# Transposing attention queries and keys before their split into two parts

## The chip, the cores and the metric

The kernel runs on one core of a Trainium2 chip. The metric is the device time of one execution in microseconds; the median of the runs shown for the kernel before is 2201.02 us.

## The reference

One trunk layer of a streaming encoder, in float32, for 2048 prompt frames and 64 frames of a running stream (2112 tokens, width 1024):

```python
a = _rmsnorm(hp, norm1)
z = a @ w_in                                   # 1024 x 2816: q, k, v of attention; q, k, v, gate of retention
qa, ka = rotate(8 heads x 64), rotate(2 kv heads x 64)
attn_o = softmax(qa ka^T / 8, with a sink per head) va    # a frame reads chunks c-2, c-1, c of 64 frames
ret_o  = chunkwise retention (4 heads x 128, decay per head)
hp = hp + concat(attn_o, rmsnorm(ret_o) * silu(gate)) @ w_out
hp = hp + relu(rmsnorm(hp) @ w_up) ** 2 @ w_down
y  = _rmsnorm(hp, norm_f)
```

It also returns the newest keys and values and the retention state of both streams. The decode stream's keys are a cache of 128 frames followed by its own 64.

## The kernel before, in words

Matrix products run on TensorE (PE) in the fast format `float32r`. To keep the precision of float32, an operand is split into a high part (a copy into float32r, on ACT) and a low part (the value less its high part, on DVE), and a product is three matmuls: high by high, high by low, low by high.

The kernel has two stretches. The first, some 730 us, does projection, attention and retention; the second the output projection and the MLP. The change is in the first. It runs over two groups `ph` of attention and retention heads (4 query heads, 1 key head and 2 retention heads each), and in each over 17 tiles of tokens: 16 of 128 and the 64 of the decode stream; 34 tiles in all. For each tile there are three projections: `z0` (384 columns: values 64, queries 256, keys 64), `z1` (512: queries and keys of the retention) and `z2` (512: its values and gates). Each is eight steps `k` of three matmuls (L584, L585, L587).

Behind each projection a first stage takes the result out of PSUM. For attention that is `att_a`: DVE and POOL rotate queries and keys into the tile `zr` [tokens, 6 blocks of 64: value, 4 queries, key] (L249), and then the whole of `zr` is split into `hl` (L254 to L256), where the high and the low part of each block stand beside each other. `vd` (L260, L261) holds copies of the split values for the scores' overlapping part.

The other stages of a tile run on PE in between the projection steps of later ones:

- `att_b` transposes `hl`: four transposes into the bank `pq` (one per query head; 128 columns are high and low part, so that the transposed head has the high part in 64 partitions and the low in the other 64), which ACT copies to `qT`; and two transposes into the bank `pk` in `keys` (high over low and low over high), which ACT copies to `kw`, the key window of this tile, and DVE to the first half of `kw_next`, that of the next tile. For the decode tile the cache's keys are split in `cache_prep` and transposed too.
- `att_c` multiplies `qT` by the two forms of `kw` (scores `s`), takes the maximum (DVE, `mx`, `ngm`) and the exponentials (ACT, L317; L321 is the sink's), and divides (DVE, L329).
- `att_d` transposes the probabilities, `idf` being the float32 identity, and splits them when it reads the banks `pt` and `pm`. `att_e` multiplies by the values, with high and low part of the values as the two halves of the stationary operand.
- `ret_b` transposes the rotated queries and keys of the retention (bank `ptr`, in float32), which DVE (`rqT`) and then ACT (`rkT`) read. `ret_c` multiplies them (`pss`). `ret_d` and `ret_e` follow.

The order of PE and of SP's queue is written out when the program is built: `run_ready` keeps a clock that counts the cost of projection steps (3 x columns x 0.4237 ns) and of stages (`COST`). A stage becomes due a time `LAT` after the stage that it needs, longer by a factor `slow` for some tiles at the ends, and is put in at the first projection step at which it is due. So `LAT` says how long ACT, DVE and POOL are trusted to take. The wait itself is done by semaphores: if they take longer, PE stands still. The order of ACT, DVE and POOL, each of which runs its instructions in a fixed order, is found by the scheduler of the framework when it builds. Two engines that read one PSUM bank do it one after the other.

Of the kernel before, what the change touches and what calls it, by code (L numbers as in the profile page):

```python
# [24 lines left out]
NT = SEQ // 128 + 1  # L25
# [14 lines left out]
def body(ctx, tc, xt, xd, xtok, w1, wout, wup, wdn, gains, sinks, ck, cv, sret, rot, rdec, qdec, dmask,  # L40
         yT, nkp, nvp, nrp, nks, nvs, nrs):
    nc = tc.nc
# [13 lines left out]
    idf = cp.tile([128, 128], F32, name="idf")  # L56
    make_identity(nc, idf)
    idr = cp.tile([128, 128], F32R, name="idr")
# [31 lines left out]
    wk = late.enter_context(tc.tile_pool(name="wk", bufs=1))  # L90
# [49 lines left out]
    def tok(t):  # L140
        return t * 128, (128 if t < NT - 1 else DEC)
# [33 lines left out]
    last_act, last_dve = [None], [None]  # L175
# [25 lines left out]
    def psum(name, dt=F32):  # L201
        return pp.tile([128, 512], dt, name=name, tag="w")
# [19 lines left out]
    def new_kw():  # L222
        return wk.tile([128, 2, 256], F32R, name="kw", bufs=2)

    def new_hl():
        return wk.tile([128, 832], F32R, name="hl", bufs=3)

    def keys(hl, T, outs):

        pk = psum("pk", F32R)  # L230
        nc.tensor.transpose(pk[:, 0:T], hl[:T, 640:768], idr[:T, :T])
        nc.tensor.transpose(pk[:, 128:128 + T], hl[:T, 704:832], idr[:T, :T])
        src = pk[:, 0:256].rearrange("p (a t) -> p a t", a=2)[:, :, :T].bitcast(F32)
        for i, o in enumerate(outs):
            if i == 0:
                nc.scalar.activation(o, src, AF.Copy)
            else:
                nc.vector.tensor_copy(o, src)

    class Att:  # L240
        pass
# [1 line left out]
    def att_a(c, ph, t, z0, rt, kw, kw_next, hl_prev):  # L243
        t0, T = tok(t)
        c.ph, c.t, c.t0, c.T, c.kw, c.kw_next, c.hl_prev, c.nch = ph, t, t0, T, kw, kw_next, hl_prev, T // 64
        zr = wk.tile([128, 6, 64], F32, name="zr")
        cs = rt[:T, 0:128].rearrange("p (a d) -> p a d", a=2)
        nc.scalar.activation(zr[:T, 0], z0[:T, 0:64], AF.Copy, scale=rs[:T, t:t + 1])
        rotate(zr[:T, 1:6], z0[:T, 64:384].rearrange("p (b d) -> p b d", d=64), T, t, 5, 64, cs)  # L249
        hl = c.hl = new_hl()  # L250
        c.vd_prev = att[ph, t - 1].vd if 0 < t < NT - 1 else None
        vd = c.vd = wk.tile([128, 2, 128], F32R, name="vd", bufs=3)
        hv = hl[:T, :768].rearrange("p (b a d) -> p b a d", a=2, d=64)
        nc.scalar.activation(hv[:, :, 0], zr[:T], AF.Copy)  # L254
        last_act[0] = nc.scalar.activation(hl[:T, 768:832], zr[:T, 5], AF.Copy)
        last_dve[0] = nc.vector.tensor_sub(hv[:, :, 1], zr[:T], hv[:, :, 0].bitcast(F32))  # L256

        for a in range(c.nch):
            v = hl[64 * a:64 * a + 64, 0:128].bitcast(F32)
            nc.scalar.activation(vd[64 * (1 - a):128 - 64 * a, a], v, AF.Copy)  # L260
            nc.vector.tensor_copy(vd[64 * a:64 * a + 64, a], v)  # L261
        with tc.issue_after(last_pool[0].ins):
            if t == NT - 2:
                nc.gpsimd.dma_start(nkp[:, ph], zr[:, 5])
                nc.gpsimd.dma_start(nvp[:, ph], zr[:, 0])
            if t == NT - 1:
                nc.gpsimd.dma_start(nks[64:128, ph], zr[:T, 5])
                nc.gpsimd.dma_start(nvs[64:128, ph], zr[:T, 0])
            if ph == 0:
                token_rest(t)  # L270

    def att_b(c):
        T, nch, hl = c.T, c.nch, c.hl
        if c.t == NT - 1:
            keys(c.hl_prev, 128, [c.kw[:, :, 0:128]])
        pq = psum("pq", F32R)
        for j in range(4):
            nc.tensor.transpose(pq[:, j * 128:j * 128 + T], hl[:T, 128 + j * 128:256 + j * 128], idr[:T, :T])
        qT = c.qT = wk.tile([128, 2, 4, 64], F32R, name="qT")
        nc.scalar.activation(qT[:, :nch].rearrange("p c h q -> p h c q"),  # L280
                             pq.rearrange("p (h c q) -> p h c q", h=4, q=64)[:, :, :nch].bitcast(F32), AF.Copy)
        outs = [c.kw[:, :, 128:128 + T]]
        if c.kw_next is not None:
            outs.append(c.kw_next[:, :, 0:128])
        keys(hl, T, outs)

    def att_c(a):
        t, g, kw, qT, nch = a.t, a.ph, a.kw, a.qT, a.nch
# [42 lines left out]
    def att_d(a):  # L331


        a.parts = [[], []]
        n, t = a.nch, a.t
        full = [c for c in range(n) if c == 1 or t > 0]
        f0, f1 = full[0] * 256, full[-1] * 256 + 256
        K = 128 if n == 2 and t > 0 else 64
        pt, pm = psum("pt"), psum("pm")
        for c in full:  # L340
            for pr in range(2):
                v = 2 * c + pr
                nc.tensor.transpose(pt[:, v * 128:v * 128 + 128], a.p[:, pr, 256 * c:256 * c + 128], idf)
        for pr in range(2):
            nc.tensor.transpose(pm[:K, pr * 128:pr * 128 + 128], a.p[:, pr, 128:128 + K], idf)
        th = wk.tile([128, 512], F32R, name="ph")
        tl = wk.tile([128, 512], F32R, name="pl")
        tm = wk.tile([128, 2, 256], F32R, name="pm")
        nc.scalar.activation(th[:, f0:f1], pt[:, f0:f1], AF.Copy)
        nc.vector.tensor_sub(tl[:, f0:f1], pt[:, f0:f1], th[:, f0:f1].bitcast(F32))  # L350
        for c in full:
            vv = (a.hl if c else a.hl_prev)[:, 0:128]
            a.parts[c] += [(vv, x[:, 256 * c:256 * c + 256]) for x in (th, tl)]
        for c in range(K // 64):
            h, l = tm[64 * c:64 * c + 64, c], tm[64 * (1 - c):128 - 64 * c, c]
            x = pm[64 * c:64 * c + 64, 0:256]
            nc.scalar.activation(h, x, AF.Copy)
            nc.vector.tensor_sub(l, x, h.bitcast(F32))
            a.parts[c].append(((a.vd_prev if c else a.vd)[:, c], tm[:, c]))

    def att_e(a):
# [101 lines left out]
    def load_cache(ph):  # L463
        cf = wk.tile([128, 2, 64], F32, name="cf")
        (nc.gpsimd if ph else nc.sync).dma_start(cf[:, 0], cv[:, ph])
        (nc.gpsimd if ph else nc.sync).dma_start(cf[:, 1], ck[:, ph])
        return cf

    def cache_prep(cf):
        hl = new_hl()  # L470
        hv = hl.rearrange("p (b d) -> p b d", d=64)
        nc.scalar.activation(hv[:, 0], cf[:, 0], AF.Copy)
        nc.vector.tensor_sub(hv[:, 1], cf[:, 0], hv[:, 0].bitcast(F32))
        nc.scalar.activation(hv[:, 10], cf[:, 1], AF.Copy)
        nc.vector.tensor_sub(hv[:, 11], cf[:, 1], hv[:, 10].bitcast(F32))
        nc.scalar.activation(hv[:, 12], cf[:, 1], AF.Copy)
# [20 lines left out]
    def do_stage(name, ph, t):  # L497
        c = att[ph, t]
        if name == "att_a":
            if (ph, t) not in kws:  # L500
                kws[ph, t] = new_kw()
            if t < NT - 2:
                kws[ph, t + 1] = new_kw()
            hl_prev = cache_prep(caches.pop(ph, None) or load_cache(ph)) if t == NT - 1 else (att[ph, t - 1].hl if t else None)
            att_a(c, ph, t, c.z[0], xs[ph, t][2], kws[ph, t], kws[ph, t + 1] if t < NT - 2 else None, hl_prev)
        elif name == "ret_a":
            ret_a(c, ph, t, c.z[1], xs[ph, t][2])
        elif name == "ret_v":
            ret_v(c, c.z[2])
        elif name == "ret_d":  # L510
            st_hist[ph, t] = ret_d(c, get_states(ph, t))
        else:
            stages[name](c)
# [15 lines left out]

    LAT = dict(z0=5.1, b_c=1.14, c_d=6.0, d_e=4.27, z1=3.56, rb_c=1.82, rc_d=1.63, z2_d=1.76, rd_e=5.0, z2_e=4.91, buf=2.43)
    COST = dict(att_b=0.35, att_c=0.85, att_d=0.66, att_e=0.72, ret_b=0.44, ret_c=0.44, ret_d=1.3, ret_e=0.22)
    clock = [0.0]
    done = {}
    queue = []
# [1 line left out]
    def ready(name, n):  # L538

        def at(st, m, lat):  # L540
            if m < 0:
                return 0.0
            return done[st, m] + LAT[lat] * slow.get(n, 1.0) if (st, m) in done else None
        need = dict(
# [11 lines left out]
    def run_ready(limit):  # L556
        while True:
# [8 lines left out]
            queue.remove(st)  # L566
            clock[0] = max(clock[0], r) + COST[st[0]]
            do_stage(st[0], st[2], st[3])
            done[st[0], st[1]] = clock[0]

    def group(ph, t, ci, n_):

        if ci == 0:
            att[ph, t] = Att()
            att[ph, t].z = {}
            queue.extend((st, n_, ph, t) for st in COST)
        xh, xl = xs[ph, t][:2]
# [35 lines left out]
    a, b = tiles[:2]  # L613
# [498 lines left out]
    for n, (p, i, d) in enumerate(steps):  # L1112
# [12 lines left out]
        o = bank()  # L1125
# [7 lines left out]
        h = {q: t[:, d] for q, t in H.items()}  # L1133
# [29 lines left out]
        if last and i in (5, 3):  # L1163
            q = 22 if i == 5 else 12
# [102 lines left out]
```

## Time and profile before

| | us |
|---|---|
| median of 3 runs (2200.22 to 2201.78) | 2201.02 |
| the profiled execution's own time | 2200.01 |
| its span, first to last instruction | 2198.2 |
| PE busy | 2177.6 |
| PE weight loads busy | 2095.8 |
| DVE busy | 1492.3 |
| ACT busy | 1141.7 |
| POOL busy | 432.2 |

Busy times are sums over the instructions of an engine. Matmuls overlap in the pipeline, so a matmul's record is longer than the place that it takes in the stream; the distance between the starts of two matmuls is that place. A wait is idle time of an engine together with the instruction that ended it.

### The profile page before, as it was taken

How to read it: one execution, taken by the hardware profiler on the slowest of the kernel's cores; microseconds unless marked ns; L12 is line 12 of the kernel's file. 1: busy time of each engine (PE TensorE's matmuls, PEld its weight loads, DVE VectorE, ACT ScalarE, POOL GpSimd, SP SyncE). 2: the span in 40 equal slices, each digit the busy share in tenths (PEclk: the TensorE clock that was granted, in tenths of full speed). 3: DMA queues.
4: the chain of work that ended last, by engine and by line, in shares of the span. 5: the costliest groups of instructions: out<-in, count | busy, mean ns of one | idle time of the engine just before them, and what ended most of it. 6: DMA issues, size and time to landing. Idle time of an engine off the chain costs nothing.

```text
span 2198.2 us, 35734 instructions
## 1 busy us (share of the span) xinstructions
PE 2177.6 (99%) x13274; PEld 2095.8 (95%) x13274; DVE 1492.3 (68%) x2560; ACT 1141.7 (52%) x2082; POOL 432.2 (20%) x481
## 2 busy tenths in 40 slices
PE   8999999999999999999999999999999999999998
PEld 7888898898888999999999999999999999999998
DVE  6565557565556576887688677666666876687665
ACT  6455455544445533555665566555545544554452
POOL 4444553444333222100000000000001200120011
PEclk9999999999999999999999999999999999999999
DMA  6567964698554789589799778666976777777662
GB/s 187 164 184 202 248 166 149 182 231 197 140 125 142 271 303 305 188 307 325 240 336 360 236 239 307 233 227 223 372 263 228 272 275 245 238 276 272 235 213 82
DMA packets 242893, 515.91 MB, mean 235 GB/s; under 512 B 21136, under 2 KB 128336, under 8 KB 238624
## 3 DMA queue, kind: packets, MB, share of 16 engines
q1 hardware_dynamic: 232192, 469.35, 62.8%
q0 software_dynamic: 8512, 43.29, 9.5%
q8 instruction: 104, 1.70, 0.3%
q10 hardware_dynamic: 2016, 1.00, 0.2%
q14 instruction: 69, 0.57, 0.1%
HBM read 411.19 MB, written 169.54 MB: 264 GB/s over the span
## 4 chain that ended last, share of the span: by engine, by line
PE 95%; DMA 2%; DVE 1%; ACT 1%; issue 1%; POOL 0%; SPq 0%; DVEq 0%; ACTq 0%; POOLq 0%
PE y L1131 10%; PE y L1130 10%; PE y L1129 10%; PE z L584 7%; PE z L585 7%; PE z L587 7%; PE b L965 4%; PE b L964 4%; PE b L963 4%; PE c L965 3%; PE a L965 3%; PE a L964 3%; PE c L964 3%; PE a L963 3%; PE c L963 3%; PE y L824 3%
## 5 line engine op out<-in xcount | busy, mean ns | idle before, releaser
L1131 PE MATMUL y<-vh,wd 128*128 128x352 f32 x1344 | 433.9, 323 | 0.0
L1130 PE MATMUL y<-vl,wd 128*128 128x352 f32 x1344 | 433.5, 323 | 0.0
L1129 PE MATMUL y<-vh,wd 128*128 128x352 f32 x1344 | 431.4, 321 | 0.0
L584 PE MATMUL z<-w,xh 128*128 128x512 f32 (+1 forms) x816 | 323.7, 397 | 0.2
L1081 POOL TENSOR_TENSOR acc<-acc,sq 128x352 f32<-128x352 f32 x41 | 71.3, 1739 | 1212.1 <-ACT sq L1080 1212.1
L585 PE MATMUL z<-w,xh 128*128 128x512 f32 (+1 forms) x816 | 306.9, 376 | 0.0
L518 ACT ACTIVATE wd<-dr 128x1024 fp32r<-128x1024 f32 x168 | 177.5, 1057 | 246.1 <-PE y L1131 167.5
L518 ACT ACTIVATE wu<-upr 128x512 fp32r<-128x512 f32 x336 | 209.2, 627 | 176.8 <-PE b L965 86.0
L587 PE MATMUL z<-w,xl 128*128 128x512 f32 (+1 forms) x768 | 288.0, 375 | 0.1
L519 DVE TENSOR_TENSOR wu<-upr,wu 128x512 fp32r<-128x512 f32 x336 | 230.7, 692 | 71.3 <-ACT wu L518 57.4
L519 DVE TENSOR_TENSOR wd<-dr,wd 128x1024 fp32r<-128x1024 f32 x168 | 209.1, 1246 | 96.6 <-ACT wd L518 96.3
L1129 PEld LDWEIGHTS y<-vh,wd 128*128 128x128 f32 x1344 | 252.5, 188 | 0.0
L1131 PEld LDWEIGHTS y<-vh,wd 128*128 128x128 f32 x1344 | 252.4, 188 | 0.0
L1130 PEld LDWEIGHTS y<-vl,wd 128*128 128x128 f32 x1344 | 251.7, 187 | 0.0
L964 PE MATMUL b<-al,wu 128*128 128x352 f32 x576 | 185.8, 323 | 0.0
L965 PE MATMUL b<-ah,wu 128*128 128x352 f32 x576 | 185.5, 323 | 0.0
L963 PE MATMUL b<-ah,wu 128*128 128x352 f32 x576 | 184.9, 321 | 0.0
L585 PEld LDWEIGHTS z<-w,xh 128*128 128x128 f32 x816 | 155.8, 191 | 16.6 <-DVE w L86 0.9
L584 PEld LDWEIGHTS z<-w,xh 128*128 128x128 f32 x816 | 155.8, 191 | 16.2 <-DVE zz L593 0.6
L519 DVE TENSOR_TENSOR vl<-rv,vh 128x1408 fp32r<-128x1408 f32 x84 | 138.2, 1647 | 41.6 <-ACT vh L518 41.1
L587 PEld LDWEIGHTS z<-w,xl 128*128 128x128 f32 x768 | 144.6, 188 | 21.9 <-DVE xl L161 0.4
L518 ACT ACTIVATE vh<-rv 128x1408 fp32r<-128x1408 f32 x84 | 116.0, 1381 | 61.9 <-DMA rv<-vscr 39.1
(295 smaller groups left out, 4770.2 us busy)
## 6 DMA issues: line engine op xcount, KB each, us to landing
rv<-vscr SPq DMA_DIRECT2D x84, 704.0 KB, 5.6
vscr<-C SPq DMA_DIRECT2D x48, 1056.0 KB, 5.8
upr<-uscr SPq DMA_DIRECT2D x192, 256.0 KB, 5.1
dr<-sscr SPq DMA_DIRECT2D x96, 512.0 KB, 4.7
upr<-in_wup SPq DMA_DIRECT2D x144, 256.0 KB, 3.5
dr<-in_wdn SPq DMA_DIRECT2D x72, 512.0 KB, 5.4
uscr<-in_wup POOLq DMA_DIRECT2D x16, 1024.0 KB, 10.0
sscr<-in_wdn POOLq DMA_DIRECT2D x16, 1024.0 KB, 9.5
```

The source lines that it names most:

```text
L518: nc.scalar.activation(h, x, AF.Copy)
L519: return nc.vector.tensor_sub(l, x, h.bitcast(F32))
L584: nc.tensor.matmul(z[:, :n], xh[:, k], wh, start=k == 0, stop=False)
L585: nc.tensor.matmul(z[:, :n], xh[:, k], wl, start=False, stop=k == NK - 1 and xl is None)
L587: nc.tensor.matmul(z[:, :n], xl[:, k], wh, start=False, stop=k == NK - 1)
L963: nc.tensor.matmul(o, wh, ah[:, k], start=k == 0 and i in (1, 6, 5), stop=False, skip_group_check=True)
L964: nc.tensor.matmul(o, wh, al[:, k], start=False, stop=False, skip_group_check=True)
L965: nc.tensor.matmul(o, wl, ah[:, k], start=False, stop=k == 3 and i in (2, 4, 3), skip_group_check=True)
L1081: nc.gpsimd.tensor_add(self.acc, self.acc, sq)
L1129: nc.tensor.matmul(o, wh, vh, start=f == 0, stop=False)
L1130: nc.tensor.matmul(o, wh, vl, start=False, stop=False)
L1131: nc.tensor.matmul(o, wl, vh, start=False, stop=f == 15)
```

## The change

Queries and keys are no longer split before the transpose. `zr` itself, in float32, is transposed: two transposes of two heads each into columns 0 to 255 of the bank `pq`, and one of the key into 64 partitions of columns 256 and up. The split is done when the bank is read: ACT copies the high parts to `kw` (twice, for its two forms) and to `qT` (once per head parity), then DVE subtracts the high parts from the bank for the low ones (twice for `kw`, twice for `qT`). The next tile's `kw_next` is a copy out of `kw`. `hl` holds only the value's two parts. `zr` has two buffers. For odd heads `qT` has the low part in the lower 64 partitions, which the sum over both forms of `kw` allows for. The cache's key is transposed straight from `cf`. In `att_d`, ACT's two reads of `pm` now come before DVE's two. The due times `z0` and `b_c` and the cost of `att_b` are changed.

```diff
     def new_hl():
-        return wk.tile([128, 832], F32R, name="hl", bufs=3)
-    def keys(hl, T, outs):
-        pk = psum("pk", F32R)
-        nc.tensor.transpose(pk[:, 0:T], hl[:T, 640:768], idr[:T, :T])
-        nc.tensor.transpose(pk[:, 128:128 + T], hl[:T, 704:832], idr[:T, :T])
-        src = pk[:, 0:256].rearrange("p (a t) -> p a t", a=2)[:, :, :T].bitcast(F32)
-        for i, o in enumerate(outs):
-            if i == 0:
-                nc.scalar.activation(o, src, AF.Copy)
-            else:
-                nc.vector.tensor_copy(o, src)
+        return wk.tile([128, 128], F32R, name="hl", bufs=3)
+    def keys(xs):
+        for x, o in xs:
+            for d in (o[0:64, 0], o[64:128, 1]):
+                nc.scalar.activation(d, x, AF.Copy)
+        yield
+        for x, o in xs:
+            for d in (o[0:64, 1], o[64:128, 0]):
+                nc.vector.tensor_sub(d, x, o[0:64, 0].bitcast(F32))
+        yield
...
-        hv = hl[:T, :768].rearrange("p (b a d) -> p b a d", a=2, d=64)
-        nc.scalar.activation(hv[:, :, 0], zr[:T], AF.Copy)
-        last_act[0] = nc.scalar.activation(hl[:T, 768:832], zr[:T, 5], AF.Copy)
-        last_dve[0] = nc.vector.tensor_sub(hv[:, :, 1], zr[:T], hv[:, :, 0].bitcast(F32))
+        last_act[0] = nc.scalar.activation(hl[:T, 0:64], zr[:T, 0], AF.Copy)
+        last_dve[0] = nc.vector.tensor_sub(hl[:T, 64:128], zr[:T, 0], hl[:T, 0:64].bitcast(F32))
...
     def att_b(c):
+        pq = psum("pq")
+        nc.tensor.transpose(pq[:64, 256:256 + T], zr[:T, 5], idf[:T, :T])
         if c.t == NT - 1:
-            keys(c.hl_prev, 128, [c.kw[:, :, 0:128]])
-        pq = psum("pq", F32R)
-        for j in range(4):
-            nc.tensor.transpose(pq[:, j * 128:j * 128 + T], hl[:T, 128 + j * 128:256 + j * 128], idr[:T, :T])
+            nc.tensor.transpose(pq[:64, 384:512], c.cf[:, 1], idf)
+        for j in range(2):
+            nc.tensor.transpose(pq[:, j * 128:j * 128 + T], zr[:T, 1 + 2 * j:3 + 2 * j].rearrange("p b d -> p (b d)"),
+                                idf[:T, :T])
+        k = keys(([(pq[:64, 384:512], c.kw[:, :, 0:128])] if c.t == NT - 1 else []) +
+                 [(pq[:64, 256:256 + T], c.kw[:, :, 128:128 + T])])
+        next(k)
         qT = c.qT = wk.tile([128, 2, 4, 64], F32R, name="qT")
-        nc.scalar.activation(qT[:, :nch].rearrange("p c h q -> p h c q"),
-                             pq.rearrange("p (h c q) -> p h c q", h=4, q=64)[:, :, :nch].bitcast(F32), AF.Copy)
-        outs = [c.kw[:, :, 128:128 + T]]
+        xs, parts = [], []
+        for h in range(2):
+            a, b = slice(64 * h, 64 * h + 64), slice(64 - 64 * h, 128 - 64 * h)
+            xs.append(pq[a, 0:256].rearrange("p (j c q) -> p j c q", j=2, q=64)[:, :, :nch])
+            parts.append([qT[r, :nch, h::2].rearrange("p c j q -> p j c q") for r in (a, b)])
+            nc.scalar.activation(parts[h][0], xs[h], AF.Copy)
+        next(k)
+        for x, (qh, ql) in zip(xs, parts):
+            nc.vector.tensor_sub(ql, x, qh.bitcast(F32))
         if c.kw_next is not None:
-            outs.append(c.kw_next[:, :, 0:128])
-        keys(hl, T, outs)
+            nc.vector.tensor_copy(c.kw_next[:, :, 0:128], c.kw[:, :, 128:256].bitcast(F32))
...
-        for c in range(K // 64):
-            h, l = tm[64 * c:64 * c + 64, c], tm[64 * (1 - c):128 - 64 * c, c]
-            x = pm[64 * c:64 * c + 64, 0:256]
+        hx = [(tm[64 * c:64 * c + 64, c], pm[64 * c:64 * c + 64, 0:256]) for c in range(K // 64)]
+        for h, x in hx:
             nc.scalar.activation(h, x, AF.Copy)
-            nc.vector.tensor_sub(l, x, h.bitcast(F32))
+        for c, (h, x) in enumerate(hx):
+            nc.vector.tensor_sub(tm[64 * (1 - c):128 - 64 * c, c], x, h.bitcast(F32))
...
-    LAT = dict(z0=5.1, b_c=1.14, c_d=6.0, d_e=4.27, z1=3.56, rb_c=1.82, rc_d=1.63, z2_d=1.76, rd_e=5.0, z2_e=4.91, buf=2.43)
-    COST = dict(att_b=0.35, att_c=0.85, att_d=0.66, att_e=0.72, ret_b=0.44, ret_c=0.44, ret_d=1.3, ret_e=0.22)
+    LAT = dict(z0=4.3, b_c=3.4, c_d=6.0, d_e=4.27, z1=3.56, rb_c=1.82, rc_d=1.63, z2_d=1.76, rd_e=5.0, z2_e=4.91, buf=2.43)
+    COST = dict(att_b=0.25, att_c=0.85, att_d=0.66, att_e=0.72, ret_b=0.44, ret_c=0.44, ret_d=1.3, ret_e=0.22)
```

## Rows read from the trace of the kernel before

**Rows 1.** The page's busy times: us (share of the span) xinstructions.
```profile
PE 2177.6 (99%) x13274; PEld 2095.8 (95%) x13274; DVE 1492.3 (68%) x2560; ACT 1141.7 (52%) x2082; POOL 432.2 (20%) x481
```
**Rows 2.** Waits of PE: who, for whom: us in total, times, longest.
```profile
PE pss L414 <- ACT rkT L408: 4.4, 2, 3.7
PE pk L231 <- DVE hl L475: 2.7, 1, 2.7
PE ptr L403 <- POOL qk L220: 1.9, 2, 1.5
```
**Rows 3.** A stretch: its us, then busy us of each engine, clock, DMA.
```profile
162.00:326.00 164.00, 164.00 (x972) 147.15 (x971) 93.73 (x262) 84.38 (x260) 83.43 (x118) 1.00 0.79 208
```
**Rows 4.** In order of time: start, us, engine, instruction; around a block of att_b.
```profile
204.25 0.46 PE L278 MATMUL pq<-idr,hl 128*128 128x128 f32 x4
...
205.02 0.40 PE L585 MATMUL z<-w,xh 128*128 128x512 f32 x1
...
205.25 0.39 PE L587 MATMUL z<-w,xl 128*128 128x512 f32 x1
```
**Rows 5.** In order of time, the block of ret_b in the same tile.
```profile
209.80 0.60 PE L403 MATMUL ptr<-idf,qk 128*128 128x128 f32 x4
...
210.47 0.39 PE L585 MATMUL z<-w,xh 128*128 128x512 f32 x1
```
**Rows 6.** Views of the tiles pm, hl, pk: count, ns least/median/most, starts, forms.
```profile
L345 PEld LDWEIGHTS pm<-idf,p x68: 110/141/143, 54.1 to 726.1; 128*128 128x128 f32 x60, 128*64 128x64 f32 x8
...
L357 ACT ACTIVATE pm<-pm x64: 361/375/382, 55.2 to 728.3; 64x256 fp32r<-64x256 f32 x64
L358 DVE TENSOR_TENSOR pm<-pm x64: 417/419/428, 56.6 to 729.7; 64x256 fp32r<-64x256 f32 x64
...
L256 DVE TENSOR_TENSOR hl<-zr,hl x34: 539/558/1960, 26.1 to 711.8; 128x384 fp32r<-128x384 f32 x32, 64x384 fp32r<-64x384 f32 x2
...
L473 DVE TENSOR_TENSOR hl<-cf,hl x2: 209/214/220, 26.0 to 677.0; 128x64 fp32r<-128x64 f32 x2
...
L236 ACT ACTIVATE kw<-pk x36: 271/379/404, 29.3 to 717.4; 128x256 fp32r<-128x256 f32 x34, 128x128 fp32r<-128x128 f32 x2
L238 DVE CAST kw<-pk x30: 410/414/425, 48.1 to 661.1; 128x256 fp32r<-128x256 f32 x30
```
**Rows 7.** In order of time, the block of att_b of the last decode tile.
```profile
716.31 0.28 PE L231 MATMUL pk<-idr,hl 128*128 128x128 f32 x1
...
717.46 0.32 PE L825 MATMUL y<-mhl,wo 128*128 128x352 f32 x1
```
**Rows 8.** In order of time, behind the block of rows 4: rotation, scores, maximum.
```profile
205.68 0.75 DVE L217 SCALAR_TENSOR_TENSOR rot<-z,rs,rt 128x512 f32<-128x512 f32 x1 [2.85 <-PE z L587]
...
206.17 0.25 PE L306 MATMUL s<-kw,qT 128*128 128x192 f32 x1
...
207.07 0.47 DVE L219 SCALAR_TENSOR_TENSOR rot<-z,rs,rt 128x256 f32<-128x256 f32 x1
...
207.29 0.40 PE L585 MATMUL z<-w,xh 128*128 128x512 f32 x1
...
207.47 1.01 DVE L313 TENSOR_REDUCE mx<-s 128x2 f32<-128x384 f32 x2
...
207.64 1.28 POOL L220 TENSOR_TENSOR qk<-rot,rot 128x512 f32<-128x512 f32 x1 [3.65 <-DVE rot L219]
```
**Rows 9.** In order of time, scores of a tile whose maximum waits for PE alone.
```profile
403.37 0.25 PE L306 MATMUL s<-kw,qT 128*128 128x192 f32 x1
...
403.99 1.02 DVE L313 TENSOR_REDUCE mx<-s 128x2 f32<-128x384 f32 x2 [1.57 <-PE s L307]
...
406.79 0.22 ACT L321 ACTIVATE es<-es 128x4 f32<-128x4 f32 x1
```
**Rows 10.** In order of time, a tile in which pss waited for rkT.
```profile
89.17 0.43 ACT L408 ACTIVATE rkT<-ptr 128x256 f32<-128x256 f32 x1
...
89.66 0.71 PE L414 MATMUL pss<-rqT,rkT 128*128 128x128 f32 x4 [0.63 <-ACT rkT L408]
```

More of the change, by code (lines that the diff above doesn't have):

```diff
@@ L245, in att_a @@
         c.ph, c.t, c.t0, c.T, c.kw, c.kw_next, c.hl_prev, c.nch = ph, t, t0, T, kw, kw_next, hl_prev, T // 64
-        zr = wk.tile([128, 6, 64], F32, name="zr")
+        zr = c.zr = wk.tile([128, 6, 64], F32, name="zr", bufs=2)
         cs = rt[:T, 0:128].rearrange("p (a d) -> p a d", a=2)
@@ L272, in att_b @@
     def att_b(c):
-        T, nch, hl = c.T, c.nch, c.hl
+        T, nch, zr = c.T, c.nch, c.zr
+        pq = psum("pq")
+        nc.tensor.transpose(pq[:64, 256:256 + T], zr[:T, 5], idf[:T, :T])
         if c.t == NT - 1:
-            keys(c.hl_prev, 128, [c.kw[:, :, 0:128]])
-        pq = psum("pq", F32R)
-        for j in range(4):
-            nc.tensor.transpose(pq[:, j * 128:j * 128 + T], hl[:T, 128 + j * 128:256 + j * 128], idr[:T, :T])
-        qT = c.qT = wk.tile([128, 2, 4, 64], F32R, name="qT")
-        nc.scalar.activation(qT[:, :nch].rearrange("p c h q -> p h c q"),
-                             pq.rearrange("p (h c q) -> p h c q", h=4, q=64)[:, :, :nch].bitcast(F32), AF.Copy)
-        outs = [c.kw[:, :, 128:128 + T]]
+            nc.tensor.transpose(pq[:64, 384:512], c.cf[:, 1], idf)
[5 more added lines that the diff above has]
+        next(k)
+        qT = c.qT = wk.tile([128, 2, 4, 64], F32R, name="qT")
+        xs, parts = [], []
[7 more added lines that the diff above has]
+            nc.vector.tensor_sub(ql, x, qh.bitcast(F32))
         if c.kw_next is not None:
-            outs.append(c.kw_next[:, :, 0:128])
-        keys(hl, T, outs)
+            nc.vector.tensor_copy(c.kw_next[:, :, 0:128], c.kw[:, :, 128:256].bitcast(F32))
     def att_c(a):
@@ L470, in cache_prep @@
         hl = new_hl()
[L471 to L476, printed above, removed]
+        nc.scalar.activation(hl[:, 0:64], cf[:, 0], AF.Copy)
+        nc.vector.tensor_sub(hl[:, 64:128], cf[:, 0], hl[:, 0:64].bitcast(F32))
         return hl
@@ L503, in do_stage @@
                 kws[ph, t + 1] = new_kw()
-            hl_prev = cache_prep(caches.pop(ph, None) or load_cache(ph)) if t == NT - 1 else (att[ph, t - 1].hl if t else None)
+            if t == NT - 1:
+                c.cf = caches.pop(ph, None) or load_cache(ph)
+            hl_prev = cache_prep(c.cf) if t == NT - 1 else (att[ph, t - 1].hl if t else None)
             att_a(c, ph, t, c.z[0], xs[ph, t][2], kws[ph, t], kws[ph, t + 1] if t < NT - 2 else None, hl_prev)
```

## The prediction

> **What bounds the kernel now.** I read the page's busy shares first, then the list of waits on PE, then the stretches, then PE in order of time around one block of transposes. The reader is to see that PE is busy in 2177.6 of 2198.2 us [rows 1], and that nearly all its waits come once: at the first tiles and at the change of head group, 4.4, 2.7 and 1.9 us [rows 2]. Between them, for instance from 162 to 326 us, PE never stands still while DVE is busy in 93.7 of 164 us [rows 3]. There each PE instruction taken out shortens the kernel by its place in the stream, and each new wait on PE lengthens it. ACT, DVE and POOL count only through the operands that PE needs next. So two questions decide: what the shorter block of transposes gives back, and whether the new order, set by the changed due times, makes PE wait.
>
> **The transposes.** A block of four pq and two pk transposes starts at 204.25; the second projection matmul behind it starts at 205.02, one undisturbed matmul takes 0.23 (205.02 to 205.25) [rows 4]. The block costs 205.02 - 204.25 - 0.23 = 0.54 us, 0.09 a transpose. Full-precision transposes are in the trace too: four of ptr from 209.80, second matmul at 210.47, so 0.67 - 0.23 = 0.44, or 0.11 each [rows 5]. A transpose out of float32 is thus a little dearer, not several times. The new block has three (two query pairs, one key): 0.33, if the key's, whose weights are 64 columns wide, costs the same. Its weight load is no longer than a full one (110 against a median of 141 ns, [rows 6]), so I take 0.11. That saves 0.21 on each of 32 full tiles, 6.7 us. The two decode tiles have eight transposes, from 716.31 to 717.46 less a slot of 352 columns, 0.16 at the pace of rows 4, = 0.99 [rows 7], and will have four, 0.44: 1.1 us for both. Sum 7.8 us. Bounds: if the new three cost only 0.09 each, 0.27 a block, the sum is 9.8; if the block came out as long as four, 0.44, it is 4.3.
>
> PE's record of one transpose is longer, 0.28 us for the pk of [rows 7], but records overlap, and the places in the stream are 0.09 to 0.11 [rows 4, 5]. The Trainium skill, page "TensorE: Matmul & The Clock Gate", section "Part 4: PE-mode transpose", gives about 275 ns for a 128x128 transpose in a kernel. Priced so, three fewer would be 0.83 a tile and over 26 us in all; the trace does not bear that out as a cost in the stream, and I go by starts.
>
> **ACT and DVE around the bank.** Before, hl was split whole (DVE 0.56) and the kw copy for the next tile came from the bank (0.41): 0.97 of DVE a tile. Now DVE splits 64 value columns (0.21), subtracts twice for the keys and twice for the queries, and copies kw for the next tile out of SBUF. A 64x256 subtraction from PSUM takes 0.42; the keys' 64x128 is not in the trace, so on the line between 64 columns (0.21) and 256 (0.42), 0.28; the copy between 0.21 and 0.41, I take 0.25. Sum 0.21 + 0.56 + 0.84 + 0.25 = 1.86, 0.9 more than before [rows 6]. Over 34 tiles that is 31 us, in a stretch where DVE is idle for four tenths of the time [rows 3]: no cost by itself, all of it if DVE became the bound. ACT, 0.38 for 64x256 and 0.27 for the smallest kw copy, has 2 x 0.27 + 2 x 0.38 = 1.30 from the bank [rows 6]. ACT reads first and DVE's subtractions wait for its last, as DVE's kw copy waited for ACT's: the chain from the transposes to the scores becomes 1.30 + 0.56 + 0.84 = 2.7.
>
> **The due times.** They move PE's order, so they are what hides this chain. One step of a projection (three matmuls of 512 columns) is 0.65 on the planner's clock, 0.69 by the rows. In a steady tile att_b now comes six steps behind the end of z0 instead of seven (4.3 for 5.1; 0.94 of other stages lie between, and 0.94 + 6 x 0.65 is the first sum above 4.3). The operand is ready sooner too: transposes read zr, not the split behind it. After att_b, two steps end z1; the scores are due 3.4 later and go in behind four steps of z2, at 2 x 0.65 + 4 x 0.65 = 3.9. In time that is 6 x 0.69 = 4.1 us for a chain of 2.7, so 1.4 are left for queueing. Behind z1, DVE has the rotation for the retention, three instructions from 205.68 to 207.54 with the 0.41 copy between, so about 1.5 [rows 8]. Should all three go ahead of the subtractions, 2.7 + 1.5 is 4.2 against 4.1: just covered. Should they stand behind, who waits is POOL's qk sum (1.28) and then ptr: DVE starts 1.3 behind att_b, has 1.4 + 0.25 + 1.5 = 3.15 to do, POOL ends at 5.8, and PE is at ptr at 4.1 + 0.89 + 0.69 = 5.7. Covered to a tenth either way; I take no cost.
>
> What comes next is closer. Before, ret_b (ptr) stood four steps behind the scores; now z1 + 3.56 falls one step behind them, and ret_c (pss) three steps behind that. The scores take 207.29 - 206.17 - 0.23 = 0.89 of PE [rows 8]. From their start to pss PE has 0.89 + 0.69 + 0.44 + 3 x 0.69 = 4.1 us, where three more steps stood between: 6.2. pss needs rkT, an ACT copy that is queued behind the four exponentials of the same tile. In a tile whose maximum is not delayed, the scores start at 403.37, DVE's maximum at 403.99 and the exponential of the sink, behind the four, at 406.79: 3.4 us behind the scores [rows 9]. With 0.22 for that one and 0.43 for rkT, rkT ends at 4.1; in front of it, at 3.9. pss follows rkT by 0.06 (89.17 + 0.43, then 89.66) [rows 10]. So PE, there at 4.1, gets it at 3.9 to 4.2: a wait of 0 to 0.1, on 17 steady tiles (those whose scores stand two or three steps behind att_b now, as in rows 4 and 8). I take 0.1 each, 1.7 us. Bounds: 0 and, with the maximum as late as it is now, 1.30 behind the scores instead of 0.62 [rows 8, 9], 0.7 to 0.8.
>
> **The rest.** att_d's reads grouped (ACT, ACT, DVE, DVE) shorten a chain on which PE does not wait: 0. At the first tiles, the wait of 2.7 for hl L475 goes, since that instruction does. Late next is ptr, which already waits 1.9 in all for POOL qk [rows 2]: PE gets there earlier and waits for it, so the net is between 2 gained and 2 lost; I take 0. The change of head group, with 3.7 lost to rkT behind weight splits [rows 2], gets another order as well: plus or minus 2, taken as 0.
>
> **Sum.** 2200.0 (the profiled execution, 1.0 under the median) - 7.8 + 1.7 = 2193.9; on the median of 2201.0 that is 2195.
>
> **Rivals.**
> 1. The gain is eaten at pss: rkT behind the exponentials costs 0.3 to 0.5 a steady tile instead of 0.1. For: the distance from scores to pss is cut by a third, and no due time knows of ACT's queue. Against: DVE is free when the scores end, if the order is as above. 17 x 0.4 = 6.8, so 2201.0 - 7.8 + 6.8 = 2200. Chance 0.27.
> 2. Slower: DVE still has its subtractions or the rotation in hand when the scores come, as it has now a rotation (maximum 1.30 behind them). Then rkT ends 0.7 later, PE waits 0.8 a steady tile, 13.6 us: 2207. It decides from 7.8 / 17 = 0.46 a tile on. For: DVE has 0.9 more a tile, all of it in the 4 us ahead of the scores. Against: the 3.15 us of such work that start 1.3 behind att_b end by 4.5, and the maximum can't start before 4.1 + 0.6. Chance 0.18.
> 3. The change doesn't do what it says: the three transposes take as long as four or more. 4.3 or less is left, so 2201.0 - 4.3 + 1.7 = 2198 and up. For: none of these shapes, 64 rows out, is in the trace. Against: [rows 5, 6]. Chance 0.05.
>
> **Chances and range.** The forecast, a gain of 4.4 to 9, has 0.50, by itself 2191 to 2197. About 0.2% (4.4 us) is what a measurement here can tell from no change. Faster by more than that: the forecast and a little of rival 1, 0.52. Within it: most of rivals 1 and 3, 0.30. Slower: rival 2, 0.18. The range runs from the cheapest transposes with no wait, 2191, less 1, to rival 2's price, 2207: 2190 to 2207.
>
> **What would show it.** In the new profile: the block of three in 0.33 by starts (step 1); the scores some six steps behind the transposes with no PE wait on DVE in front of them; DVE near 1.9 a tile for these lines. PE's list of waits tells the rest: no pss row beyond a few us in total is the forecast, 5 to 8 there is rival 1, over 12 rival 2. I am wrong if PE waits at a place that I have costed at nothing, the scores for qT or att_e, or if PE's waits at the first tiles grow by more than 2 us.

## The result and the profile after

The changed kernel takes 2209.71 us (median of 4 runs, 2208.48 to 2210.52), the kernel before 2200.62 beside it (2200.14 to 2201.78): a ratio of 1.0038, 95% interval 1.0027 to 1.005. By the ratio that is 8.4 us slower (the two medians are 9.1 apart), where 6 us faster was forecast; the median lies 2.7 us above the upper end of the range. The profiled execution took 2208.48, its span is 2206.7.

PE is busy as long as before [rows 1], although it has 104 instructions fewer; DVE has 28 us more. The page's busy times after:

```profile
PE 2177.2 (99%) x13170; PEld 2085.6 (95%) x13170; DVE 1520.5 (69%) x2698; ACT 1140.6 (52%) x2114; POOL 424.7 (19%) x481
```

The list of PE's waits is where the two kernels part (who, for whom: us in total, times, longest). Before, pss stood first with 4.4, pk with 2.7 followed, ptr had 1.9 [rows 2]. After, ptr has 9.1, two waits for the high and the low part of an input tile (`xh`, `xl`) and one for the exponentials `p` are new, and pss is down to 0.9:

```profile
PE ptr L411 <- POOL qk L220: 9.1, 3, 6.8
PE z L590 <- ACT xh L160: 1.9, 1, 1.9
PE z L593 <- POOL xl L161: 1.9, 1, 1.9
...
PE pst L437 <- ACT p L325: 1.1, 1, 1.1
PE pss L422 <- ACT rkT L416: 0.9, 2, 0.7
```

In the long stretch of [rows 3] PE now has 0.16 us of waits and DVE 105.1 us of work for 93.7 (columns: stretch, its us, busy us of PE, its weight loads, DVE, ACT, POOL, granted clock, DMA share, GB/s):

```profile
162.00:326.00 164.00, 163.84 (x945) 143.29 (x944) 105.10 (x304) 87.44 (x281) 79.57 (x117) 1.00 0.80 213
```

**One steady tile**, in order of time (start, us, engine, line, instruction), the tile that answers to [rows 4, 5 and 8]:

```profile
208.99 0.27 PE L272 MATMUL pq<-idf,zr 128*64 128x128 f32 x1
209.10 0.38 PE L276 MATMUL pq<-idf,zr 128*128 128x128 f32 x2
209.52 0.55 ACT L232 ACTIVATE kw<-pq 64x128 fp32r<-64x128 f32 x2 [0.93 <-PE pq L276]
...
209.55 0.39 PE L591 MATMUL z<-w,xh 128*128 128x512 f32 x1
...
210.08 0.77 ACT L288 ACTIVATE qT<-pq 64x256 fp32r<-64x256 f32 x2
...
210.89 0.58 DVE L236 TENSOR_TENSOR kw<-pq,kw 64x128 fp32r<-64x128 f32 x2 [1.83 <-PE z L593]
...
211.39 0.84 DVE L291 TENSOR_TENSOR qT<-pq,qT 64x256 fp32r<-64x256 f32 x2
212.27 0.75 DVE L217 SCALAR_TENSOR_TENSOR rot<-z,rs,rt 128x512 f32<-128x512 f32 x1
...
213.46 0.25 PE L314 MATMUL s<-kw,qT 128*128 128x192 f32 x1
...
213.90 1.27 POOL L220 TENSOR_TENSOR qk<-rot,rot 128x512 f32<-128x512 f32 x1 [3.46 <-DVE rot L219]
...
215.22 0.42 PEld L411 LDWEIGHTS ptr<-idf,qk 128*128 128x128 f32 x4 [0.45 <-POOL qk L220]
215.22 0.65 PE L411 MATMUL ptr<-idf,qk 128*128 128x128 f32 x4
215.63 0.47 PE L590 MATMUL z<-w,xh 128*128 128x512 f32 x1
215.95 0.39 PE L591 MATMUL z<-w,xh 128*128 128x512 f32 x1
```

The block of three transposes costs 209.55 - 208.99 - 0.23 = 0.33 us, as forecast. DVE's first subtraction starts at 210.89, just behind ACT's last read of the bank (210.08 + 0.77 = 210.85), so the rotation, whose input was ready some 0.7 earlier, starts at 212.27 only; POOL's sum ends at 215.17, and PE, free for ptr at 215.04 (the matmul before it started at 214.81 and has a place of 0.23), starts at 215.22. The first weight load of the block (PEld) starts with it; before, it starts 0.23 ahead of the matmul at 209.80 [rows 5]:

```profile
209.57 0.59 PEld L403 LDWEIGHTS ptr<-idf,qk 128*128 128x128 f32 x4
```

The wait of 0.18 is too short for the list of waits. The view of the tile ptr has it: between 203 and 324 us, six tiles, this is what PE and its weight loads stood idle for in front of ptr (us, times); before, the same view has no such line. From 483 to 672 us, nine tiles, it is 4.0.

```profile
  POOL qk L220: 2.7, 6
```

**Where the 8 us went.** For each PE instruction I took the distance to the start before it, less its undisturbed place (0.23 us for 512 columns, 0.17 for 384, 0.16 for 352, about 0.11 for the short ones), and summed what is over 0.08, by stretches (the same us of each trace). It is worked out from the starts in the traces (us; the kernels of the last three columns are experiments below):

| stretch | before | after | rt in three buffers | rotation first | all four mends |
|---|---|---|---|---|---|
| 0 to 45, first tiles | 12.3 | 16.8 | 18.4 | 11.5 | 11.4 |
| 45 to 203, irregular tiles | 5.3 | 8.6 | 9.1 | 8.0 | 8.8 |
| 203 to 324, steady tiles | 2.5 | 4.1 | 4.2 | 4.2 | 3.1 |
| 324 to 385, change of head group | 6.2 | 9.9 | 3.2 | 11.1 | 5.2 |
| 385 to 483, irregular tiles | 2.1 | 3.3 | 3.8 | 3.4 | 3.3 |
| 483 to 672, steady tiles | 4.0 | 6.2 | 6.4 | 6.3 | 4.8 |
| 672 to 706 | 1.5 | 0.9 | 0.9 | 0.9 | 1.0 |
| sum | 33.9 | 49.8 | 46.0 | 45.4 | 37.6 |

After less before is 15.9; the transposes' 7.8 off it leaves 8.1, against 8.5 between the two spans. So the gain came, and four losses of 3.7 to 4.5 us each ate it twice over: first tiles 4.5, irregular tiles 4.5, steady tiles 3.8, change of head group 3.7. Each column is one execution, and its sums are good to 1 or 2 us: for the last three columns the same reckoning gives 4.3, 3.7 and -4.1, where the spans differ by 2.3, 4.0 and -6.2. At 45 us the lag on the kernel before is 4.0 in the changed kernel and 6.3 in experiment 3, whose edit leaves the first tiles alone.

### The profile page after: what moved, and what is told of

The parts are those of the page before. It is cut to its first block, busy times and chain, and to the rows that moved or that the text cites. A ratio compares the mean times of both kernels' runs of the same rounds, so it can differ in the third digit from the quotient of the medians.

```text
span 2206.7 us, 35748 instructions
## 1 busy us (share of the span) xinstructions
PE 2177.2 (99%) x13170; PEld 2085.6 (95%) x13170; DVE 1520.5 (69%) x2698; ACT 1140.6 (52%) x2114; POOL 424.7 (19%) x481
## 4 chain that ended last, share of the span: by engine, by line
PE 79%; DMA 1%; DVE 0%; ACT 0%; issue 0%; SPq 0%; POOL 0%; DVEq 0%; ACTq 0%
PE y L1137 10%; PE y L1136 10%; PE y L1135 9%; PE b L971 4%; PE b L970 4%; PE b L969 4%; PE z L590 3%; PE z L591 3%; PE z L593 3%; PE y L830 3%; PE y L832 3%; PE y L831 3%; PE a L971 3%; PE a L970 3%; PE a L969 3%; PE c L971 3%
```

## The experiments

Differences are (ratio - 1) x 2200.6, against the kernel before run beside each; the interval of a ratio is 0.001 to 0.0014 to either side, 2 to 3 us. On this scale the changed kernel is at +8.4.

**1 and 2. The two halves of the change alone.**

```diff
 # in the changed kernel: due times of before
-LAT = dict(z0=4.3, b_c=3.4, ...);  COST = dict(att_b=0.25, ...)
+LAT = dict(z0=5.1, b_c=1.14, ...); COST = dict(att_b=0.35, ...)
 # in the kernel before: the opposite edit
```

> The changed kernel with the due times and costs of before, so the new way through the bank alone. Theory (the chain of 2.7 us from the transposes to the scores, DVE's four subtractions at its end, is what the due times have to cover): scores come two or three steps, 1.4 to 2.1 us, behind the transposes and PE waits 0.6 to 1.3 us for qT in most of 32 tiles, 20 to 40 us: 2220 to 2240. Rival (the new due times themselves are what costs, the data path is cheap): 2193 to 2200.

Measured 2274.38, ratio 1.0331 (1.0317 to 1.0345), +73. PE's waits name it:

```profile
PE s L314 <- DVE qT L291: 41.7, 21, 2.3
```

> The kernel before with the new due times and costs alone. Theory (DVE's subtractions ahead of the rotation make ptr late, not the place of the stages): no ptr wait in steady tiles, no shorter transposes, 2198 to 2204, with what the new order does at the first tiles and the head group as the only difference. Rival (the new order itself costs what the change lost, about 9 us plus the 8 that the transposes gave): 2209 to 2218.

Measured 2201.13, ratio 0.9998 (0.9989 to 1.0007). The new order costs nothing beyond the interval with the old data path, and the new data path needs the new order: 2.0 us of wait in each of 21 tiles without it. That is more than the 0.6 to 1.3 expected, and the time is 34 us above the upper end of the theory's range: the direction was right, the size was not. The list of waits is not all of the 73: from 203 to 324 us the granted clock is 0.93 in this run and 1.00 in the changed kernel.

**3. ptr later in the steady tiles.**

```diff
-return done[st, m] + LAT[lat] * slow.get(n, 1.0) ...
+late = 4.2 if lat == "z1" and n not in slow else LAT[lat]
+return done[st, m] + late * slow.get(n, 1.0) ...
```

> The changed kernel with a later due time for the ptr transposes (4.2 for 3.56) in the steady tiles alone, one step of a projection later. Theory (in steady tiles the 0.2 us that the transposes give is eaten by a ptr wait of 0.18 and the weight load behind it): the ptr block falls from 0.67 to 0.44, and the lag against the kernel before falls by 0.2 a steady tile over some 20 tiles: 2205 to 2206. Rival (the next wait in line, rkT at pss, takes its place, or the gain is lost elsewhere): 2208 to 2211.

Measured 2206.08, ratio 1.0021 (1.0012 to 1.003): 3.7 us back. In five steady tiles, from 205.5 to 307.8 us of the kernel before, its lag on the same projection matmul falls from 8.39 to 7.25 us, 0.23 a tile, while the changed kernel's goes from 5.22 to 5.36. One step more of distance shows the 0.21 of the transposes; no other wait took its place in these tiles. One of 1.3 us, pr for DVE's `sd`, is new at 496 us.

**4. The key in a bank of its own.**

```diff
-nc.tensor.transpose(pq[:64, 256:256 + T], zr[:T, 5], idf[:T, :T])
+pk = psum("pk")
+nc.tensor.transpose(pk[:64, 0:T], zr[:T, 5], idf[:T, :T])
```

> The changed kernel with the key's transpose in a bank of its own, as pk had before. Theory (DVE's subtractions are late because they stand behind ACT's last read of the one bank, and with them the rotation and POOL's qk): the key subtractions start 0.5 to 0.8 us earlier behind the transposes, the rotation of the steady tiles starts at the end of z1 instead of 0.7 behind it, and the ptr waits go, 0.2 a tile and part of those at 85 and 129 us: 2203 to 2206. Rival (the query subtractions still wait for ACT's last copy, so all ends nearly as late, or the bank is missed elsewhere): 2208 to 2211.

Measured 2205.74, ratio 1.0022 (1.0013 to 1.0031): 3.5 us back. The same tile, in order of time:

```profile
211.06 0.27 PE L273 MATMUL pk<-idf,zr 128*64 128x128 f32 x1
...
211.37 0.56 ACT L232 ACTIVATE kw<-pk 64x128 fp32r<-64x128 f32 x2 [0.71 <-PE pk L273]
...
211.95 0.77 ACT L289 ACTIVATE qT<-pq 64x256 fp32r<-64x256 f32 x2
211.96 0.58 DVE L236 TENSOR_TENSOR kw<-pk,kw 64x128 fp32r<-64x128 f32 x2 [0.83 <-ACT kw L232]
212.75 0.86 DVE L292 TENSOR_TENSOR qT<-pq,qT 64x256 fp32r<-64x256 f32 x2 [0.21 <-ACT qT L289]
...
213.95 0.75 DVE L217 SCALAR_TENSOR_TENSOR rot<-z,rs,rt 128x512 f32<-128x512 f32 x1
...
215.57 1.28 POOL L220 TENSOR_TENSOR qk<-rot,rot 128x512 f32<-128x512 f32 x1 [3.07 <-DVE rot L219]
...
217.11 0.60 PE L412 MATMUL ptr<-idf,qk 128*128 128x128 f32 x4
```

DVE starts 0.90 behind the transposes instead of 1.90 and subtracts the keys while ACT still reads the queries. POOL ends 5.79 behind them instead of 6.18, PE is there at 6.05, and the idle time in front of ptr from 203 to 324 us is gone; the waits at 88 and 132 us (0.7 and 1.7) stayed, though a part of them was expected to go. The Trainium skill, page "PSUM — Partial Sum Buffer", section "PSUM bank collisions raise a hardware error", says that two engines must not touch the same 32 partitions of one bank at the same time, and gives a semaphore by bank as the simple version of the rule. The two traces agree with the simple version: DVE begins 0.04 behind ACT's last read of the shared bank, though that read is of the other 64 partitions, and 0.03 behind the key copies once the key has its own.

**5. The first tiles, two edits that gain little.** POOL's split of the third tile's input put behind the qk sums, and the due times of before for the first two tiles:

```diff
+with tc.issue_after(last_pool[0].ins):          # 5a, for the third tile
     nc.gpsimd.tensor_sub(l, xr[:, a, :T], h.bitcast(F32))
```
```diff
+first = dict(z0=5.1, b_c=1.14) if n < 2 else {} # 5b
+return done[st, m] + first.get(lat, LAT[lat]) * slow.get(n, 1.0) ...
```

> The changed kernel with one instruction moved: POOL's split of the third tile's input (2.34 us) goes behind the two qk sums of the first two tiles, as it stood before. Theory (the first ptr waits 6.8 us because this split went in front of qk): the longest ptr wait falls from 6.8 to about 4.5, 2.0 to 4.5 us back in all (the granted clock falls behind the long wait): 2205 to 2208. Rival (the start is lost to DVE's subtractions in front of the rotation, or whatever POOL does first the later matmuls wait for the split): 2209 to 2210.

> The changed kernel with the due times of before for the transposes and scores of the first two tiles alone. Theory (the 4.5 us lost by 43 us come from the earlier place of the first transposes, whose subtractions then go in front of the rotation): the first ptr wait of 6.8 shrinks and the lag at 43 us is 1 to 2 us, as in the run with all due times of before: 2206 to 2207.5. Rival (the data path itself costs that at the start): lag 4 to 5, 2209 to 2210.

Measured 2208.10, ratio 1.0033 (1.002 to 1.0045), and 2210.29, ratio 1.0046 (1.0033 to 1.0059): neither differs from the changed kernel by more than the intervals. With the split behind the sums the longest ptr wait falls from 6.8 to 4.5, about what the split takes on POOL. But in that trace PE waits 1.5 us for the first tile's cached key (0.2 in the changed kernel), the rotation that ptr needs runs 2.0 later, at 34.54 instead of 32.53, and ptr starts only 0.3 earlier. Among the other runs with the new transposes this wait for the key is between nothing and 1.6 us, so what 5a is worth by itself stays open. With the old due times for these tiles, ptr still waits about 5 us and the scores 2.7 more: the loss changes its place and stays.

**6. The first tile's rotation first.** The order of work at the start of the changed kernel, in order of time:

```profile
24.36 0.68 DVE L599 TENSOR_TENSOR zz<-z,zb 64x512 f32<-64x512 f32 x1
...
25.26 3.01 POOL L194 TENSOR_SCALAR rsv<-rd,rs 64x4 f32<-64x4 f32 x1
...
25.89 2.06 DVE L86 SCALAR_TENSOR_TENSOR w<-waraw,gsb,w 128x512 fp32r<-128x512 f32 x3
...
30.08 0.58 DVE L291 TENSOR_TENSOR qT<-pq,qT 64x128 fp32r<-64x128 f32 x2
30.51 0.59 POOL L184 TENSOR_TENSOR rs<-ms,mhalf 128x1 f32<-128x1 f32 x1
...
31.48 0.55 DVE L217 SCALAR_TENSOR_TENSOR rot<-z,rs,rt 128x320 f32<-128x320 f32 x1
...
32.53 0.73 DVE L217 SCALAR_TENSOR_TENSOR rot<-zz,rs,rt 64x512 f32<-64x512 f32 x1
...
35.22 2.34 POOL L161 TENSOR_TENSOR xl<-xr,xh 128x1024 fp32r<-128x1024 f32 x1
...
37.52 2.54 POOL L220 TENSOR_TENSOR qk<-rot,rot 64x512 f32<-64x512 f32 x2
38.82 0.69 PE L411 MATMUL ptr<-idf,qk 64*128 64x64 f32 x4 [6.82 <-POOL qk L220]
```

The rotation of zz, which PE's ptr waits for, has its operand at 25.0 and runs at 32.53: on DVE it stands behind the subtractions of the first transposes and behind the next tile's rotation, which cannot start before POOL's rs at 31.1. In the kernel before it ran at 31.76, behind the next tile's rotation too:

```profile
31.76 0.73 DVE L217 SCALAR_TENSOR_TENSOR rot<-zz,rs,rt 64x512 f32<-64x512 f32 x1
...
35.63 0.46 PE L403 MATMUL ptr<-idf,qk 64*128 64x64 f32 x4 [1.48 <-POOL qk L220]
```

So ptr starts 3.2 us later than before: 0.8 because the rotation is later, and 2.3 because POOL splits the next input (`xl`) in front of its sum. PE is there 2.2 earlier than before (32.00 for 34.15), since the wait of 2.7 for hl is gone. The experiment emits that next tile's att_a after the first tile's ret_a:

```diff
-do_stage(("att_a", "ret_a", "ret_v")[ci], ph, t)
+if (n_, ci) != (1, 0):
+    do_stage(("att_a", "ret_a", "ret_v")[ci], ph, t)
+if (n_, ci) == (0, 1):
+    do_stage("att_a", *tiles[1])
```

> The changed kernel with the rotation of the first tile's retention heads put ahead of the next tile's first rotation on DVE; the transposes stay where they are. Theory (that rotation's operand is there 8 us before it runs; it stands in DVE's order behind a rotation that waits for POOL's rs, and behind the new subtractions, and POOL's qk and the first ptr follow it): the first ptr wait of 6.8 falls under 2, the lag against before at 43 us falls from 4.5 to 0 to 1.5, 2204.5 to 2206.5. Rival (PE is held by another operand at the start, the split or the weights, so the wait only moves): lag 3 or more, 2208 to 2210.

Measured 2203.97, ratio 1.0011 (1.0002 to 1.002): 5.9 us back, a little more than expected: at 45 us the lag on the kernel before goes from 4.0 to -1.7. The rotation runs early, ptr does not wait:

```profile
26.74 0.73 DVE L217 SCALAR_TENSOR_TENSOR rot<-zz,rs,rt 64x512 f32<-64x512 f32 x1
...
28.36 1.34 POOL L220 TENSOR_TENSOR qk<-rot,rot 64x512 f32<-64x512 f32 x1 [0.21 <-DMA dm<-in_dmask]
...
34.45 0.46 PE L411 MATMUL ptr<-idf,qk 64*128 64x64 f32 x4
```

Whether the same edit would have helped the kernel before as much:

> The kernel before with the rotation of the first tile's retention heads put ahead of the next tile's first rotation on DVE, the same edit that gave 5.7 us back in the changed kernel. Theory (before, the late rotation cost PE only 1.9 us at the first ptr, and the wait for hl of 2.7 stays): 0 to 2.5 us gained, 2198.5 to 2201. Rival (the edit is worth as much in any order of the stages, so it says nothing about the change): 4 to 6 gained, 2195 to 2197.

Measured 2203.63 beside 2200.52, ratio 1.0013 (1.0004 to 1.0022): slower by 3. Both expectations are missed. Before, PE comes to the first pk transposes with DVE's hl still to be done, and the rotation put ahead of it made that wait of 2.7 one of 5.1. So the edit pays in the changed kernel alone: before, the rotation is late as well, but another operand is late first.

**7. Three buffers for rt.** At the change of head group, the queue of SP and the rotation that frees rt, after and then before:

```profile
340.36 0.48 DVE L219 SCALAR_TENSOR_TENSOR rot<-z,rs,rt 128x256 f32<-128x256 f32 x1
...
340.86 0.33 SPq L171 DMA_DIRECT2D rt<-in_rot  x1
...
341.24 17.49 SPq L117 DMA_DIRECT2D raw<-in_w  x11
```
```profile
333.00 0.48 DVE L219 SCALAR_TENSOR_TENSOR rot<-z,rs,rt 128x256 f32<-128x256 f32 x1
...
333.50 0.33 SPq L171 DMA_DIRECT2D rt<-in_rot  x1
...
333.88 13.55 SPq L117 DMA_DIRECT2D raw<-in_w  x11
```

SP stands at the load of rt until DVE's rotation has let go of the buffer, and eleven weight loads stand behind it. After, they start 7.4 us later and take 3.9 longer. Of the 7.4, 5.5 is the lag that the kernel has by then; in the remaining 1.9 DVE's subtractions stand in front of the rotation, from 337.92 to 339.26.

```diff
-rt = xp.tile([128, 384], F32, name="rt")
+rt = xp.tile([128, 384], F32, name="rt", bufs=3)
```

> The changed kernel with three buffers instead of two for the rotation table rt. Theory (at the change of head group SP's queue stands at the load of rt until DVE's late rotation gives the buffer free, and the 11 weight loads behind it come 7 us later): weight loads start several us earlier, the waits for xh and xl (2.1 and 2.1) go, the lag grows by 0 to 1 us instead of 2 to 3 between 326 and 483: 2206 to 2207.5. Rival (the raw buffers and DVE's splits set the pace, not the load of rt): 2209 to 2210.

Measured 2204.44, ratio 1.0016 (1.0007 to 1.0024): 4.8 us back, more than expected. The loads start at 327.74, and the waits for xh and xl shrink to one of 0.8:

```profile
327.08 0.61 SPq L171 DMA_DIRECT2D rt<-in_rot  x1
327.74 18.08 SPq L117 DMA_DIRECT2D raw<-in_w  x11
```

In the table the stretch from 324 to 385 falls from 9.9 to 3.2, below the kernel before, whose SP waits there too: 14.5 us from the end of its last issue to the load of rt, against 15.8 in the changed kernel. So the edit mends more than the change lost. Whether the kernel before would gain by a third buffer was not tried.

**8. The reads of pm in the old order.** The order of the four reads, not the code itself:

```diff
-ACT, ACT, DVE, DVE
+ACT, DVE, ACT, DVE
```

> The changed kernel with the reads of pm in att_d in the old order (ACT, DVE, ACT, DVE). Theory (PE does not wait on this chain): within 1.5 us of the changed kernel, 2208 to 2211. Rival (two ACT reads in a row and two subtractions in a row push the rotation back and are part of the loss): 2205 to 2207.

Measured 2210.12, ratio 1.0036 (1.0024 to 1.0049): no difference from the changed kernel. This part of the change is worth nothing either way.

**9. The mends together.** Three (5b, 3 and 7), then two (4 and 7), then four (4, 7, 6 and 5a), then these four with ptr later in two irregular tiles:

```diff
+late = {3: 1.3, 5: 2.6}.get(n, 0.0) if lat == "z1" else 0.0   # the last one
```

> The changed kernel with three of the mends together: due times of before for the first two tiles, the later ptr of the steady tiles, three buffers for rt. Theory (the three losses are separate and add up): 3.6 for the steady tiles, 2 to 3 at the start, 2 to 3 at the change of head group, so 2200 to 2203, about the time of before. Rival (what one mend gives another takes, as one order feeds the next): 2204 to 2207.

> The changed kernel with the key's transpose in a bank of its own and three buffers for rt. Theory (the two losses, DVE late in every steady tile and SP's queue held at the head group, are separate): 4.0 and 5.3 us add up, 2199 to 2202. Rival (with the key's bank the rotation comes earlier and frees rt in time, so the two mend the same thing): 2203 to 2205.

> The changed kernel with the key's own bank, three buffers for rt, the first rotation ahead and the split of the third tile's input behind the qk sums. Theory (all that the change lost beside its shorter transposes is these places, so that with them mended the 7.8 us of the transposes show): 2194 to 2198, faster than before by 0.15 to 0.35%. Rival (the losses in the irregular tiles at 85 and 129 us and others keep it at the time of before): 2199 to 2202.

> The changed kernel with all mends and, for two irregular tiles, later due times for ptr (by 1.3 and 2.6). Theory (the ptr waits of 0.8 at 79 and 1.9 at 125 us are there because these tiles' rotations stand on DVE behind att_d's subtractions): both waits go, 1.5 to 3 us, 2192 to 2194. Rival (the stages moved behind them meet other waits there, as with the scores at 170 us in the run of three mends): 2195 to 2197.

| | us | ratio to before | 95% interval | us against before |
|---|---|---|---|---|
| 5b, 3, 7 | 2200.91 | 1.0000 | 0.9992 to 1.0009 | 0 |
| 4, 7 | 2200.41 | 0.9993 | 0.9984 to 1.0002 | -1.5 |
| 4, 7, 6, 5a | 2195.05 | 0.9971 | 0.996 to 0.9982 | -6.4 |
| the same, ptr later | 2192.29 | 0.9965 | 0.9953 to 0.9978 | -7.7 |

The four mends gave 3.5, 4.8, 5.9 and 1.1 alone, 15.3 in all, and 14.7 together, as if the losses were separate. (Each of the four is counted from the same +8.4, whose interval is 5.9 to 11.0, so an error in it enters the 15.3 four times and the 14.7 once.) (In the first row 5b adds nothing again: 3 and 7 alone are worth 8.5, the row 8.4.) With them the kernel is faster than before by 6.4 us (4.0 to 8.8). PE's waits then begin with

```profile
PE ptr L413 <- POOL qk L221: 2.4, 2, 1.8
```

and these are the two at 79 and 125 us that the last kernel removes. One of them returned as a wait at pss of 1.6 at 129 us, so both theory and rival of that run hold in part, and its gain of 1.3 lies within the intervals. How the rest of the irregular tiles' 4.5 us splits up was not settled.

## Why the prediction was wrong

The steps that failed are those that booked a place at nothing. By the table PE lost time at four such places, 3.8 us in the steady tiles, 4.5 in the first, 3.7 at the change of head group and 4.5 in the irregular tiles, twice the 7.8 gained; the sum had 1.7, for a wait that did not come.

- **The transposes: right.** 0.33 a block was forecast and measured, and experiment 3 shows it in the time.
- **The prices on ACT and DVE: right.** Median 283 ns for the keys' subtraction (0.28 forecast), 409 for the queries' (0.42), 269 and 378 for ACT's reads (0.27 and 0.38); only the copy for the next tile was dearer, 285 for 250.
- **"Covered to a tenth either way; I take no cost": the step that failed in the steady tiles.** The sum in front of it, POOL at 5.8 and PE at ptr at 5.7 behind the transposes, is right to a few hundredths: from the end of the block at 209.32, POOL ends at 5.85 and PE is free at 5.72. Two of its terms are off by a quarter of a us and cancel: DVE starts 1.57 behind, not 1.3, since ACT's first read comes 0.2 late; and the copy for the next tile (0.29) runs behind the rotation, not in front. What was wrong is to book a shortfall of 0.1 as nothing. PE waits 0.18, and the block behind the wait takes 215.95 - 215.22 - 0.23 = 0.50 instead of 0.44 [rows 5], where the first weights were not loaded ahead: 0.24 a tile, which is more than the 0.21 gained. Experiment 3 measured it at 0.23 + 0.03 = 0.26 a tile, and 4 took it away from the other side.
- **The pss waits for rkT, 1.7 us: wrong.** There are none in the steady tiles; the whole list has 0.9 for pss. In the tile above rkT ends 3.92 behind the start of the scores and pss starts at 4.34, so the lower of the two times forecast, 3.9, was the right one.
- **The first tiles, "between 2 gained and 2 lost; I take 0": 4.5 lost.** It was argued by one wait that goes and one that is late next. What was not followed is the order of DVE and POOL: the subtractions came to stand in front of a rotation that ptr waits for (0.8 us), and POOL's split in front of the sum behind it (2.3), while PE came 2.2 earlier.
- **The change of head group, "plus or minus 2, taken as 0": 3.7 lost.** The path went over an engine that was not in the argument: DVE's rotation frees rt, SP's queue stands at its load, and the weights come late. Experiment 7 shows the path, but not that it is all of the 3.7, as it mends a wait that the kernel before has too. More DVE work in a tile was costed by the operands that PE needs, not by the buffers that it frees for transfers.
- **The irregular tiles had no term** and lost 4.5. Two ptr waits, 0.9 and 1.4, are part of it; the rest stays open.
- **The rivals.** Rival 2's time, 2207, is the nearest, and its premise, DVE still at the subtractions when the next work comes, is right. Its place is wrong: it let pss pay by way of the maximum, and the payer is ptr by way of the rotation. Its test, over 12 us at pss, would have read as refuted. The last sentence on what would be wrong, a wait "at a place that I have costed at nothing" or more than 2 us at the first tiles, is what came, though the places that it named there, the scores and att_e, were not the ones.

## What to carry to other kernels

Where an edit gives PE a little in every tile and lengthens a chain on another engine, add that chain from its first event, with every queueing step, and give each cover of a tenth or two a price of its own: a wait of 0.18 us in each tile is too short for a list of waits and still eats the gain. Follow an engine's added work also to the buffers that it frees, for a queue that issues in order, as SP's does here, turns one late release into late loads for everything behind it. When a sound change comes out slower, look for the one-off places in its new order before giving it up; here four small edits turned +8.4 us into -6.4, one of them by way of a wait that the kernel before has as well.

## What the runs showed of the hardware

- After PE's wait of 6.82 us at ptr, matmuls of 512 columns follow each other at 0.43 us instead of 0.23, from 40.0 to 42.6 us. The granted clock is 0.81 from 20 to 40 us and 0.93 from 40 to 60 in the changed kernel; with the rotation first both are 1.00. So part of what the rotation first gives back is clock, time at the lower of the two levels (1.2 GHz). Little of the 4.5 lost against the kernel before is clock: behind its wait of 2.7 that kernel too has them at 0.43, from 31.4 to 33.5 us, and a granted clock of 0.91 and 1.00. The rows of the changed kernel, then the first one of the kernel before:

```profile
20.00:40.00 20.00, 11.43 (x48) 8.12 (x47) 17.75 (x34) 12.22 (x30) 16.06 (x20) 0.81 0.61 193
40.00:60.00 20.00, 20.00 (x100) 16.32 (x99) 5.95 (x20) 7.61 (x25) 6.21 (x10) 0.93 0.09 27
```
```profile
20.00:40.00 20.00, 15.73 (x69) 11.82 (x68) 16.42 (x31) 12.93 (x31) 13.72 (x20) 0.91 0.60 195
```

- DVE and POOL take longer beside each other. POOL's rsv of 64x4 took 3.01 us at 25.26, where its median is 0.30, and ended 0.3 behind DVE's row of three weight splits (25.89 to 27.95); in the run of 5a, at 26.61 and clear of that row, it took 0.61. DVE's copies vd at 36.17, beside POOL's xl and qk, took 2.75 for two; in the kernel before the same two, at 37.26 while POOL stood idle, took 0.46. DVE's row of three splits took 2.06 in the changed kernel and 3.11 with the rotation first, where POOL's sum of 1.34 ran beside it. The Trainium skill, page "GPSIMD Engine Reference", section "Specifications", says that the two share their SBUF interfaces and contend when DVE runs in a 2-port mode or has two SBUF inputs; the splits have two and agree with it, the copies have one, and no row shows their mode.
